# W_o of a hybrid retention block by seven products, its weight sums made in DRAM

## The chip, the cores and the metric

One core of one Trainium2 chip runs the whole layer in one launch. The metric is the device time of that launch in microseconds (us), the median of several runs. The engines are named as in the profile: PE is TensorE, DVE is VectorE, ACT is ScalarE, POOL is GpSimd, SP is SyncE, which here only issues DMAs.

## The reference

The layer takes x (512 tokens by 1024 features, float32). What matters for this change is the step that ends the token mixers:

```python
merged = jax.nn.sigmoid(gate_a) * y_a + jax.nn.sigmoid(gate_r) * y_r
x = x + merged @ w_o[l]                     # w_o: 1024 x 1024
h2 = rmsnorm(x, g_ffn[l])
x = x + (jax.nn.silu(h2 @ w_ff_gate[l]) * (h2 @ w_ff_up[l])) @ w_ff_down[l]
```

`y_a` is the output product of the short convolution (W_a_out, 1024 x 1024), `y_r` that of the retention (W_r_out, 2048 x 1024). In front of them stands one wide input projection; behind `x` comes the feed-forward part and a last RMSNorm.

## The kernel before, in words

**Precision.** All products are float32 by pairs: an operand t is held as hi (t rounded to the fast format) and lo = t - hi, and a product is the three matmuls hi·hi, hi·lo, lo·hi (`mm3`, L339 to L341; L380 and L424 in the other helpers). A weight piece of 128 x 1024 is loaded into a raw tile, ACT writes hi (L200), DVE writes lo (L201). There are ten raw tiles and five pairs of hi and lo; `take` keeps at least two pieces made ahead of the product that consumes them (AHEAD = 2), and their loads are issued four plan entries ahead (LEAD = 4).

**Seven products for eight.** Most of the projections are done by Winograd's form of Strassen's algorithm: both operands are cut into 2 x 2 quadrants, four sums of quadrants are formed on each side (s1 to s4 of the activations, t1 to t4 of the weights), and seven products of quadrants take the place of eight. `strassen` (L434 to L458) does it for token-major outputs: the products a11, s1, s2, a12, s3, a22, s4 in that order, each by `prod_tm` with 2 weight pieces and 24 matmuls of 512 columns, in three pairs of PSUM banks (a, d, b; there are eight banks). The weight sums t1 to t4 are made in SBUF by DVE adds (L298), except for the first two feed-forward quads (SUMMED), whose sums POOL's DMAs make in DRAM: a copy, then accumulating transfers (`sum_step`). There each of these is pinned behind a store of the same stage with `issue_after`.

**Order.** PLAN lists the weight pieces in order of consumption. The program is written in one order, and a list scheduler at build time may move an instruction ahead of others on its engine as soon as its inputs and its buffer are there; on the chip each engine runs its own list in order. Large activations live in fourteen `big` tiles.

**Around the change.** After the last product of W_r_out, `strassen(4, zf, ...)` computes y_a; its evictions `merge` (L967 to L971) multiply by the gate (L970) and add y_r (L971), behind the combining adds of `strassen` (L445, L450, L457). `turn(half)` (L974 to L984) transposes one half of the merged features, 16 transposes on PE, and splits them (L200, L201). W_o itself is not done by seven products: two halves of columns by two blocks of rows by four k by four token blocks, three matmuls each, all in eight banks; its last block is split into a `big` tile (`inbig`). The first two blocks run for all tokens, then each token block nb is finished in turn: `ev_o` (L999 to L1018) adds x (L1003), writes the row to DRAM, squares it on ACT (L1006) and scales it for the FFN (L1015); `tr_o` (L1020 to L1035) transposes it one block later (L1030) into the feed-forward operand. The feed-forward part starts with five products that need only the first 256 tokens (`first_tokens`); its own sums of activations come from `form` (L1162 to L1165: one DVE operation, one ACT cast, one DVE subtraction).

Of the kernel before, what the change touches and what calls it, by code (L numbers as in the profile page):

```python
# [53 lines left out]
WIDTH = {"w": 512, "x": 256, "a": 512, "f": 256, "d": 512}  # L54
# [96 lines left out]
SUMMED = (("f", 0), ("f", 1))  # L151


def loads():


    out = []
    for i, x in enumerate(PLAN):
        if x[0] == "q":
            _, quad, name, u, nk = x  # L160
            need = name if quad in SUMMED else NEEDS.get(name)
            if need:
                out.append((i, quad, need, u, nk * WIDTH[quad[0]]))
    return out + [(len(PLAN), quad, "b12", 0, 4 * WIDTH[quad[0]]) for quad in SUMMED]

# [6 lines left out]
def block_kernel(ctx: ExitStack, tc: tile.TileContext, xw0, xw, xT, xtok, wpack, wquad, cols, decs, rot, g_ffn, g_final, out):  # L172
# [51 lines left out]
    def unit(inbig=False):  # L224
        if inbig:
            t = bigtile(F32R)
            return t[:, 0:2, :].rearrange("p a b -> p (a b)"), t[:, 2:4, :].rearrange("p a b -> p (a b)")
# [4 lines left out]
    def prefetch_block(loads, splits, inbig):  # L232
# [8 lines left out]
        for c in range(2):  # L241
            hi, lo = unit(inbig)
# [8 lines left out]
    wsum = {(quad, f): dram.tile([P, QH], F32, name=f"{f}{quad[0]}{quad[1]}")  # L251
            for quad in SUMMED for f in ("t1", "t2", "t3", "t4")}

    def quarter(quad, name, u=0):
        return wquad[next(i for i, x in enumerate(QUARTERS) if x[1:4] == (quad, name, u))]

    steps = [(quad, f, g, add) for group in (
        (("t1", "b11", 0), ("t3", "b22", 0)), (("t1", "b12", 1), ("t3", "b12", 1)),
        (("t2", "t1", 0),), (("t2", "b22", 1),), (("t4", "t2", 0),), (("t4", "b21", 1),))
        for quad in SUMMED for f, g, add in group]  # L260

    def sum_step(behind=None):

        if steps:
            quad, f, g, add = steps.pop(0)
            src = wsum[quad, g] if g[0] == "t" else quarter(quad, g)
# [11 lines left out]
    def load_raws(upto):  # L278
        while loaded[0] < len(LOADS) and LOADS[loaded[0]][0] <= upto:
            _, quad, name, u, n = LOADS[loaded[0]]  # L280
            t = rawtile()
            src = wsum[quad, name] if name[0] == "t" else quarter(quad, name, u)
# [20 lines left out]
    def prefetch(first=False, loads=None, splits=None):  # L303
# [7 lines left out]
        if x[0] == "c":  # L311
            units = prefetch_block(loads, splits, x[1] == "w_o" and x[2] == 512 and x[4] == 512)
# [121 lines left out]
    def strassen(n, forms, ev11, ev21, ev22, ev12):  # L434
# [366 lines left out]
    def do_mix(s):  # L801
        us, c = [], bigtile()[:, 0:2, :]
        feature_major(xg, lambda m, ps: us.append(snap(ps)))
# [7 lines left out]
        def ev_b(m, ps):  # L811
            nc.vector.tensor_tensor(out=c[:, m], in0=ps, in1=c[:, m], op=ALU.mult)
        feature_major(xg, ev_b)
# [102 lines left out]
    def do_wr(h, yr):  # L916
# [3 lines left out]
        for half in range(2):  # L920
            def ev(nb, ps):
# [5 lines left out]
                if h == HEADS - 1:  # L927
                    nc.vector.tensor_tensor(out=t, in0=t, in1=sgr[half][:, nb, :], op=ALU.mult)
            token_major(yr, 0, 1, ev)
# [34 lines left out]
    mt = ([], [])  # L964

# [8 lines left out]
    def turn(half):  # L974
        hi, lo = bigtile(F32R), bigtile(F32R)
        mt[0].append(hi)
        mt[1].append(lo)
        for nb in range(NB):
# [6 lines left out]
    strassen(4, zf, merge(0, 0), merge(0, 2), merge(1, 2), merge(1, 0))  # L985
    turn(0)


# [8 lines left out]
    XF, xf32 = {}, {}  # L997

    def ev_o(nb, pss):  # L999
        ac = small.tile([P, 6], F32, tag="fin", name="ac")  # L1000
        for half in range(2):
            yt = y[half][:, nb, :]
            nc.vector.tensor_tensor(out=yt, in0=pss[half], in1=yt, op=ALU.add)  # L1003
            nc.sync.dma_start(ydr[nb * P:(nb + 1) * P, half * 512:(half + 1) * 512], yt)
            sq = t512()
            nc.scalar.activation(sq, yt, AF.Square, accum_out=ac[:, half:half + 1])  # L1006
        nc.vector.tensor_scalar(out=ac[:, 3:4], in0=ac[:, 0:1], scalar1=1.0 / D, scalar2=EPS,
                                op0=ALU.mult, op1=ALU.add)
# [3 lines left out]
        hs = []  # L1012
        for half in range(2):
            h = t512()
            nc.vector.scalar_tensor_tensor(out=h, in0=y[half][:, nb, :], scalar=ac[:, 5:6],  # L1015
                                           in1=gb[:, half * 512:(half + 1) * 512], op0=ALU.mult, op1=ALU.mult)
            hs.append(h)
        return hs  # L1018

    def tr_o(nb, hs):  # L1020
# [6 lines left out]
        for q in range(2):  # L1027
            ps = bank()
            for k in range(4):
                nc.tensor.transpose(ps[:, k * P:(k + 1) * P], hs[q][:, k * P:(k + 1) * P], ident)  # L1030
# [6 lines left out]
    po = [[bank() for _ in range(NB)]]  # L1037
    for half in range(2):
        c = Chunk()
        for k in range(4):  # L1040
            for nb in range(NB):
                mm3(po[half][nb], act_pair(mt, k, slice(nb * P, (nb + 1) * P)), c.w(k, 0, 512), k == 0, False)
        if half == 0:
            turn(1)
            po.append([bank() for _ in range(NB)])
    cs = [Chunk(), Chunk()]
    hs = [None] * NB
    for nb in range(NB):
        for half in range(2):
            for k in range(4):  # L1050
                mm3(po[half][nb], act_pair(mt, 4 + k, slice(nb * P, (nb + 1) * P)), cs[half].w(k, 0, 512),
                    False, k == 3)
        if nb:
            tr_o(nb - 1, hs[nb - 1])
        hs[nb] = ev_o(nb, [po[half][nb] for half in range(2)])
        if nb in (1, 3):

            prefetch()
# [103 lines left out]
    def form(name, o, in0, in1, op):  # L1162
        nc.vector.tensor_tensor(out=o, in0=in0, in1=in1, op=op)
        XF[name] = form_tile()
        split(o, *XF[name])  # L1165
# [5 lines left out]
    form("s1", a22, a21, a22, ALU.subtract)  # L1171
    first_tokens(*FIRST_PRODUCTS[2])
    form("s2", a22, a22, a11, ALU.subtract)
    first_tokens(*FIRST_PRODUCTS[3])
    form("s3", a21, a11, a21, ALU.subtract)
    first_tokens(*FIRST_PRODUCTS[4])
    form("s4", a12, a12, a22, ALU.add)
# [116 lines left out]
def pack_quads(w_in, w_a, gate, up, down):  # L1294

    out = np.zeros((len(QUARTERS), P, QH), np.float32)
    for i, (_, (kind, *q), name, u, n) in enumerate(QUARTERS):
# [3 lines left out]
        elif kind == "a":  # L1301

            w = w_a.reshape(4, 2, P, 2, 512)[u:u + n // 512, r, :, c]
        elif kind == "f":
# [50 lines left out]
```

## Time and profile before

| what | value |
|---|---|
| median of 3 runs | 1027.11 us (1026.5 to 1027.32) |
| the profiled execution, its own time | 1027.93 us |
| its span, first to last instruction | 1026.1 us |
| busy PE, DVE, ACT, POOL | 1018.1, 886.3, 535.5, 125.0 us |
| mean granted PE clock | 0.999 of 2.4 GHz |

Busy time of PE counts overlapping matmuls as one stretch, so a busy PE need not run at its peak. The chain of waits is followed back from the last instruction and says which engine set the end. A wait of an engine off that chain costs nothing by itself.

### The profile page before, as it was taken

To read this page: it belongs to the slowest core of one execution; us is meant where nothing else is said; L and a number is where in the kernel's file an instruction comes from. 1 tells how busy PE (TensorE), PEld (TensorE's weight loads), DVE (VectorE), ACT (ScalarE), POOL (GpSimd) and SP (SyncE) were. 2 spreads that over 40 slices of the span, in tenths; PEclk is the share of its full clock that TensorE was granted. 3 is DMA by queue.
4 is the path that set the end of the run, shared out by engine and by line. 5 is a ranking of instruction groups with operands and counts; after the bars stand their busy time and mean duration, and the time that the engine had idled before them with its cause. 6 is when DMAs were issued, how large, how long until landed. Compare 5 with 4: busy or idle time off the path is not lost.

```text
span 1026.1 us, 14780 instructions
## 1 busy us (share of the span) xinstructions
PE 1018.1 (99%) x5610; PEld 887.9 (87%) x5610; DVE 886.3 (86%) x1151; ACT 535.5 (52%) x728; POOL 125.0 (12%) x205
## 2 busy tenths in 40 slices
PE   9999999999999999999999999999999999999997
PEld 7888888888888998888888888889998999899986
DVE  7878998969798988797999998569998999889996
ACT  7547655553656455342542334356654565556554
POOL 0030231222212003202011000000002000110011
PEclk9999999999999999999999999999999999999999
DMA  9525597794767657828177525633318522663513
GB/s 346 195 83 183 172 299 211 213 312 153 255 203 238 254 200 256 323 81 314 52 277 285 208 94 176 236 102 121 122 44 220 177 87 83 193 156 103 164 29 96
DMA packets 51304, 187.66 MB, mean 183 GB/s; under 512 B 6880, under 2 KB 7008, under 8 KB 47264
## 3 DMA queue, kind: packets, MB, share of 16 engines
q1 hardware_dynamic: 36448, 133.19, 37.5%
q0 software_dynamic: 14496, 53.23, 17.5%
q8 instruction: 44, 0.72, 0.3%
q10 hardware_dynamic: 288, 0.29, 0.1%
q14 instruction: 28, 0.23, 0.1%
HBM read 148.14 MB, written 46.92 MB: 190 GB/s over the span
## 4 chain that ended last, share of the span: by engine, by line
PE 97%; DVE 1%; DMA 1%; issue 0%; POOL 0%; ACT 0%; POOLq 0%; DVEq 0%; ACTq 0%
PE bank L424 34%; PE bank L380 28%; PE bank L339 11%; PE bank L341 11%; PE bank L340 11%; DMA raw<-wquad 1%; PE bank L470 0%; PE bank L1030 0%; PE bank L981 0%; PE bank L655 0%; DVE wlo L201 0%; DVE raw L298 0%; DVE big L1229 0%; DVE t L445 0%; POOL fin L1219 0%
## 5 line engine op out<-in xcount | busy, mean ns | idle before, releaser
L200 ACT CAST whi<-raw 128x1024 fp32r<-128x1024 f32 (+2 forms) x291 | 294.5, 1028 | 278.7 <-PE bank L424 60.0
L201 DVE TENSOR_TENSOR wlo<-raw,whi 128x1024 fp32r<-128x1024 f32 (+2 forms) x292 | 343.9, 1193 | 81.6 <-ACT whi L200 81.1
L380 PE MATMUL bank<-xform,whi 128*128 128x256 f32 x1424 | 257.6, 284 | 0.2 <-ACT whi L200 0.2
L380 PEld LDWEIGHTS bank<-xform,whi 128*128 128x128 f32 x1424 | 222.4, 192 | 1.2 <-ACT t L431 0.5
L380 PE MATMUL bank<-xform,wlo 128*128 128x256 f32 x712 | 201.5, 283 | 0.0
L424 PE MATMUL bank<-whi,big 128*128 128x512 f32 x596 | 187.6, 390 | 0.0
L298 DVE TENSOR_TENSOR raw<-raw 128x1024 f32<-128x1024 f32 (+1 forms) x128 | 152.1, 1206 | 3.8 <-DMA raw<-wquad 2.8
L380 PEld LDWEIGHTS bank<-xform,wlo 128*128 128x128 f32 x712 | 136.8, 192 | 0.0
L424 PEld LDWEIGHTS bank<-whi,big 128*128 128x128 f32 x596 | 112.0, 188 | 23.8 <-ACT t L431 0.4
L424 PE MATMUL bank<-whi,xform 128*128 128x512 f32 x384 | 121.3, 390 | 0.0
L424 PE MATMUL bank<-wlo,big 128*128 128x512 f32 x298 | 116.2, 390 | 0.0
L431 ACT COPY t<-bank 128x512 f32<-128x512 f32 x105 | 61.0, 585 | 56.3 <-PE bank L380 29.7
L339 PE MATMUL bank<-big,whi 128*128 128x512 f32 x220 | 85.8, 390 | 0.0
L341 PE MATMUL bank<-big,wlo 128*128 128x512 f32 x220 | 85.7, 390 | 0.0
L340 PE MATMUL bank<-big,whi 128*128 128x512 f32 x220 | 85.7, 390 | 0.0
L424 PEld LDWEIGHTS bank<-whi,xform 128*128 128x128 f32 x384 | 72.1, 188 | 15.1 <-DVE xform L201 0.2
L424 PE MATMUL bank<-wlo,xform 128*128 128x512 f32 x192 | 74.8, 390 | 0.0
L339 PE MATMUL bank<-whi,big 128*128 128x512 f32 x176 | 69.0, 392 | 0.0
L340 PE MATMUL bank<-wlo,big 128*128 128x512 f32 x176 | 68.6, 390 | 0.0
L341 PE MATMUL bank<-whi,big 128*128 128x512 f32 x176 | 68.2, 390 | 0.0
L424 PEld LDWEIGHTS bank<-wlo,big 128*128 128x128 f32 x298 | 56.0, 188 | 11.4
L340 PEld LDWEIGHTS bank<-big,whi 128*128 128x128 f32 x220 | 41.3, 188 | 8.6
(205 smaller groups left out, 1394.8 us busy)
## 6 DMA issues: line engine op xcount, KB each, us to landing
raw<-wquad SPq DMA_DIRECT2D x132, 512.0 KB, 4.6
raw<-wpack SPq DMA_DIRECT2D x50, 512.0 KB, 5.3
z<-t POOLq DMA_DIRECT2D x24, 256.0 KB, 4.7
zform<-z POOLq DMA_DIRECT2D x6, 1024.0 KB, 6.0
v<-t POOLq DMA_DIRECT2D x16, 256.0 KB, 5.3
sg<-t POOLq DMA_DIRECT2D x16, 256.0 KB, 5.0
qh<-t POOLq DMA_DIRECT2D x16, 256.0 KB, 3.0
ql<-t POOLq DMA_DIRECT2D x16, 256.0 KB, 3.6
```

The source lines that it names most:

```text
L200: first = (round or nc.scalar.copy)(hi, src)
L201: nc.vector.tensor_tensor(out=lo, in0=src, in1=hi.bitcast(F32), op=ALU.subtract)
L298: nc.vector.tensor_tensor(out=t, in0=t, in1=raws[quad, more, u][:, 0:n], op=ALU.add)
L339: nc.tensor.matmul(ps, lh, rh, start=first, stop=False)
L340: nc.tensor.matmul(ps, lh, rl, start=False, stop=False)
L341: nc.tensor.matmul(ps, ll, rh, start=False, stop=last)
L380: nc.tensor.matmul(o, l[:, c], r[:, k], start=start and s == 0 and k == 0 and i == 0, stop=stop and k == 3 and i == 2, skip_group_check=True)
L424: nc.tensor.matmul(pss[tt], l, r[:, c], start=start and k == 0 and i == 0, stop=stop and k == n - 1 and i == 2, skip_group_check=True)
L431: nc.scalar.copy(t, ps)
```

## The change

W_o goes over to seven products of 24 matmuls, with its weight sums t1 to t4 made in DRAM by POOL's transfers as for the first two feed-forward quads: 16 more transfers, of which only the first two fall into calls of `sum_step` that pin them. `strassen` gets a hook `behind`, through which the convolution's output product now does three things between its own products: before a22 the quadrant a11 of the merged features is transposed; before s4 (its last) the quadrant a22 is transposed, W_o's first product a11 is run, quadrant a21 is transposed and s1 is formed. `strassen` of W_a_out moves behind the load of `y` (x token-major) in the program. The rest of W_o follows: s1, s2, a12, s4, s3, a22; each result is added to y by `join`, and `complete` does what `ev_o` did, token block by token block. Of the four `tr_o` two now stand before the first feed-forward product and two between the first three. `inbig` and the two explicit `prefetch` calls are dropped. `form` is the function of before with the dictionary as an argument.

```diff
-WIDTH = {"w": 512, "x": 256, "a": 512, "f": 256, "d": 512}
+WIDTH = {"w": 512, "x": 256, "a": 512, "o": 512, "f": 256, "d": 512}
...
-    for name in FORMS:
+    for kind, name in [("a", x) for x in FORMS[:6]] + [("o", "b11"), ("a", "b22")] + [
+            ("o", x) for x in ("t1", "t2", "b21", "b22", "t3", "t4")]:
         for u in (0, 2):
-            out.append(("q", ("a",), name, u, 2))
-    for r in (0, 512):
-        for c in (0, 512):
-            b("w_o", r, 4, c, 512)
+            out.append(("q", (kind,), name, u, 2))
...
-SUMMED = (("f", 0), ("f", 1))
+SUMMED = (("f", 0), ("f", 1), ("o",))
+
+
+def parts(quad):
+    return (0, 2) if quad == ("o",) else (0,)
...
-    steps = [(quad, f, g, add) for group in (
+    steps = [(quad, f, g, u, add) for quads in (SUMMED[:2], SUMMED[2:]) for group in (
         (("t1", "b11", 0), ("t3", "b22", 0)), (("t1", "b12", 1), ("t3", "b12", 1)),
         (("t2", "t1", 0),), (("t2", "b22", 1),), (("t4", "t2", 0),), (("t4", "b21", 1),))
-        for quad in SUMMED for f, g, add in group]
+        for quad in quads for f, g, add in group for u in parts(quad)]
...
-            with tc.issue_after(behind.ins):
+            with tc.issue_after(behind.ins) if behind else nullcontext():
                 if add:
-                    nc.gpsimd.dma_start(out=wsum[quad, f], in_=src, accum_op=ALU.add, max_dma_last_dim=4 * CH)
+                    nc.gpsimd.dma_start(out=wsum[quad, f, u], in_=src, accum_op=ALU.add, max_dma_last_dim=4 * CH)
                 else:
-                    nc.gpsimd.dma_start(wsum[quad, f], src)
+                    nc.gpsimd.dma_start(wsum[quad, f, u], src)
...
-    def strassen(n, forms, ev11, ev21, ev22, ev12):
+    def strassen(n, forms, ev11, ev21, ev22, ev12, behind=None):
...
+        if behind:
+            behind(5)
         prod_tm(n, forms["a22"], a, False, True)
         for tt in range(2):
             ev21(tt, a[tt])
+        if behind:
+            behind(6)
         prod_tm(n, forms["s4"], d, False, True)
...
     def do_mix(s):
         us, c = [], bigtile()[:, 0:2, :]
+        if s == 3:
+            sum_step()
+            sum_step()
...
+            sum_step()
+            sum_step()
             token_major(yr, 0, 1, ev)
...
+    def turn(half, th):
+        name = f"a{th + 1}{half + 1}"
...
+        if name != "a21":
+            M[name] = form_tile()
+        for tt in range(2):
             ps = bank()
             for k in range(4):
-                nc.tensor.transpose(ps[:, k * P:(k + 1) * P], sga[half][:, nb, k * P:(k + 1) * P], ident)
+                nc.tensor.transpose(ps[:, k * P:(k + 1) * P], sga[half][:, 2 * th + tt, k * P:(k + 1) * P], ident)
             ps = ps.rearrange("p (k t) -> p k t", k=4)
-            sl = slice(nb * P, (nb + 1) * P)
-            split(ps, hi[:, :, sl], lo[:, :, sl])
+            sl = slice(tt * P, (tt + 1) * P)
+            if name != "a21":
+                split(ps, *(t[:, :, sl] for t in M[name]))
+            nc.scalar.copy(m32[name][:, :, sl], ps)
+
+    def form(out, name, o, in0, in1, op):
+        nc.vector.tensor_tensor(out=o, in0=in0, in1=in1, op=op)
+        out[name] = form_tile()
+        split(o, *out[name])
...
+    def join(nb, half, ps, op=ALU.add):
+
+        yt = y[half][:, nb, :]
+        nc.vector.tensor_tensor(out=yt, in0=yt, in1=ps, op=op)
+
+    def complete(nb, half, last):
+        yt, ac = y[half][:, nb, :], acs[nb]
+        nc.sync.dma_start(ydr[nb * P:(nb + 1) * P, half * 512:(half + 1) * 512], yt)
+        nc.scalar.activation(t512(), yt, AF.Square, accum_out=ac[:, last:last + 1])
...
+    def behind(i):
+        if i == 5:
+            turn(0, 0)
+            return
+        turn(1, 1)
+        po["a"] = [bank(), bank()]
+        prod_tm(4, of(M["a11"]), po["a"], True, False, lambda tt: join(tt, 0, po["a"][tt]))
+        turn(0, 1)
+        form(M, "s1", m32["a22"], m32["a21"], m32["a22"], ALU.subtract)
+    strassen(4, zf, merge(0, 0), merge(0, 2), merge(1, 2), merge(1, 0), behind)
+    a, d, b = po["a"], [bank(), bank()], [bank(), bank()]
+    prod_tm(4, of(M["s1"]), d, True, False, lambda tt: join(2 + tt, 1, d[tt]))
+    form(M, "s2", m32["a22"], m32["a22"], m32["a11"], ALU.subtract)
+    turn(1, 0)
+    prod_tm(4, of(M["s2"]), a, False, False, lambda tt: join(tt, 1, a[tt], ALU.subtract))
+    form(M, "s4", m32["a12"], m32["a12"], m32["a22"], ALU.add)
...
+    prod_tm(4, of(M["a12"]), b, True, True, ev)
+    form(M, "s3", m32["a21"], m32["a11"], m32["a21"], ALU.subtract)
...
+    prod_tm(4, of(M["s4"]), d, False, True, ev)
...
+    prod_tm(4, of(M["s3"]), a, False, False, ev)
...
+    prod_tm(4, of(M["a22"]), a, False, True, ev)
...
     first_tokens(*FIRST_PRODUCTS[0])
+    tr_o(2)
     first_tokens(*FIRST_PRODUCTS[1])
-    tr_o(NB - 1, hs[NB - 1])
+    tr_o(3)
```

## Rows read from the trace of the kernel before

**Rows 1.** The page: span, and the busy time of each engine.

```profile
span 1026.1 us, 14780 instructions
PE 1018.1 (99%) x5610; PEld 887.9 (87%) x5610; DVE 886.3 (86%) x1151; ACT 535.5 (52%) x728; POOL 125.0 (12%) x205
```

**Rows 2.** The page's chain that ended last, by engine.

```profile
PE 97%; DVE 1%; DMA 1%; issue 0%; POOL 0%; ACT 0%; POOLq 0%; DVEq 0%; ACTq 0%
```

**Rows 3.** All waits of PE: who for whom, us in total, times, longest.

```profile
PE bank L470 <- DVE t L467: 1.4, 1, 1.4
PE bank L380 <- ACT whi L200: 0.2, 1, 0.2
```

**Rows 4.** The chain in order of time, longest pieces: start us, us, what.

```profile
1.45 4.45 PE bank L470 x10
...
602.38 38.08 PE bank L424 x168
640.46 1.75 PE bank L981 x16
...
677.61 0.87 PE bank L1030 x8
...
690.71 5.75 PE bank L380 x48
```

**Rows 5.** Groups of PE from 640.2 to 690.8, one of three lines.

```profile
L340 PE MATMUL bank<-wlo,big 128*128 128x512 f32 x48 | 18.8, 391 | 0.0
...
L340 PE MATMUL bank<-big 128*128 128x512 f32 x16 | 6.2, 390 | 0.0
```

**Rows 6.** Stretches: us, busy PE, PEld, DVE, ACT, POOL; PEclk, DMA share, GB/s.

```profile
602.20:640.30 38.10, 38.10 (x170) 31.51 (x169) 31.60 (x39) 17.93 (x20) 0.00 (x0) 1.00 0.41 134
640.30:690.70 50.40, 50.40 (x251) 41.72 (x250) 30.11 (x46) 22.25 (x40) 1.64 (x3) 1.00 0.50 173
```

**Rows 7.** Stretches of 5 us in the same columns.

```profile
632.00:637.00 5.00, 5.00 (x24) 4.14 (x23) 5.00 (x9) 2.11 (x2) 0.00 (x0) 1.00 0.50 183
...
662.00:667.00 5.00, 5.00 (x23) 4.13 (x22) 1.23 (x1) 1.05 (x1) 0.00 (x0) 1.00 0.55 190
```

**Rows 8.** Timeline of DVE, end of W_a_out: start us, us, what.

```profile
623.67 1.28 DVE L445 TENSOR_TENSOR t<-bank,t 128x512 f32<-128x512 f32 x2
624.87 1.28 DVE L970 TENSOR_TENSOR big<-t,big 128x512 f32<-128x512 f32 x2
...
627.28 2.36 DVE L201 TENSOR_TENSOR wlo<-raw,whi 128x1024 fp32r<-128x1024 f32 x2
629.55 1.37 DVE L450 TENSOR_TENSOR t<-bank,t 128x512 f32<-128x512 f32 x2
```

**Rows 9.** Groups from 596 to 700: the ACT cast of a weight piece.

```profile
L200 ACT CAST whi<-raw 128x1024 fp32r<-128x1024 f32 x24 | 25.1, 1052 | 44.8 <-PE bank L341 21.6 <-PE bank L424 15.7 <-DVE big L928 4.4
```

**Rows 10.** Timeline of DVE at the feed-forward part's forms.

```profile
700.02 2.47 DVE L1163 TENSOR_TENSOR big<-big 128x1024 f32<-128x1024 f32 x2
...
708.68 3.49 DVE L201 TENSOR_TENSOR xform<-big,xform 128x1024 fp32r<-128x1024 f32 x3
```

**Rows 11.** Timeline of SP and of POOL: an early load, a gap.

```profile
528.55 0.33 SPq L1193 DMA_DIRECT2D gf<-g_final  x1
...
381.08 0.72 POOL L626 DMA_DIRECT2D z<-t  x1 [52.08 <-ACT t L200]
```

**Rows 12.** DMA issues: count, KB each, median us to landing.

```profile
t1f<-wquad POOLq DMA_DIRECT2D x4, 512.0 KB, 7.7
...
t2f<-wquad POOLq DMA_DIRECT2D x2, 512.0 KB, 9.3
```

**Rows 13.** The first 20 us in stretches, columns as in rows 6.

```profile
0.00:10.00 10.00, 8.55 (x27) 5.21 (x28) 5.61 (x15) 5.82 (x11) 0.72 (x7) 1.00 0.82 281
10.00:20.00 10.00, 10.00 (x46) 8.29 (x45) 9.90 (x16) 9.46 (x17) 0.00 (x0) 1.00 1.02 405
```

**Rows 14.** Timeline of ACT, the first weight casts that wait for a load.

```profile
19.48 1.05 ACT L200 CAST whi<-raw 128x1024 fp32r<-128x1024 f32 x1 [0.54 <-DMA raw<-wpack]
```

More of the change, by code (lines that the diff above doesn't have):

```diff
@@ L1 @@
-from contextlib import ExitStack
+from contextlib import ExitStack, nullcontext
 import numpy as np
@@ L163, in loads @@
                 out.append((i, quad, need, u, nk * WIDTH[quad[0]]))
-    return out + [(len(PLAN), quad, "b12", 0, 4 * WIDTH[quad[0]]) for quad in SUMMED]
+    return out + [(len(PLAN), quad, "b12", u, QH) for quad in SUMMED for u in parts(quad)]
 LOADS = loads()
@@ L222, in block_kernel, with unit @@
     ready = []
[L224 to L227, printed above, removed]
+    def unit():
         hi = wpool.tile([P, QH], F32R, tag="whi", name="whi")
@@ L230, in unit, with prefetch_block @@
         return hi, lo
-    def prefetch_block(loads, splits, inbig):
+    def prefetch_block(loads, splits):
         i = block[0]
@@ L241, in prefetch_block @@
         for c in range(2):
-            hi, lo = unit(inbig)
+            hi, lo = unit()
             units.append((hi, lo))
@@ L249, in block_kernel, with quarter @@
     raws = {}
-    wsum = {(quad, f): dram.tile([P, QH], F32, name=f"{f}{quad[0]}{quad[1]}")
-            for quad in SUMMED for f in ("t1", "t2", "t3", "t4")}
-    def quarter(quad, name, u=0):
+    wsum = {(quad, f, u): dram.tile([P, QH], F32, name="_".join(map(str, (f, u, *quad))))
+            for quad in SUMMED for u in parts(quad) for f in ("t1", "t2", "t3", "t4")}
+    def quarter(quad, name, u):
         return wquad[next(i for i, x in enumerate(QUARTERS) if x[1:4] == (quad, name, u))]
-    steps = [(quad, f, g, add) for group in (
+    steps = [(quad, f, g, u, add) for quads in (SUMMED[:2], SUMMED[2:]) for group in (
         (("t1", "b11", 0), ("t3", "b22", 0)), (("t1", "b12", 1), ("t3", "b12", 1)),
         (("t2", "t1", 0),), (("t2", "b22", 1),), (("t4", "t2", 0),), (("t4", "b21", 1),))
-        for quad in SUMMED for f, g, add in group]
+        for quad in quads for f, g, add in group for u in parts(quad)]
     def sum_step(behind=None):
         if steps:
-            quad, f, g, add = steps.pop(0)
-            src = wsum[quad, g] if g[0] == "t" else quarter(quad, g)
-            with tc.issue_after(behind.ins):
+            quad, f, g, u, add = steps.pop(0)
+            src = wsum[quad, g, u] if g[0] == "t" else quarter(quad, g, u)
+            with tc.issue_after(behind.ins) if behind else nullcontext():
                 if add:
-                    nc.gpsimd.dma_start(out=wsum[quad, f], in_=src, accum_op=ALU.add, max_dma_last_dim=4 * CH)
+                    nc.gpsimd.dma_start(out=wsum[quad, f, u], in_=src, accum_op=ALU.add, max_dma_last_dim=4 * CH)
                 else:
-                    nc.gpsimd.dma_start(wsum[quad, f], src)
+                    nc.gpsimd.dma_start(wsum[quad, f, u], src)
     def rawtile():
@@ L281, in load_raws @@
             t = rawtile()
-            src = wsum[quad, name] if name[0] == "t" else quarter(quad, name, u)
+            src = wsum[quad, name, u] if name[0] == "t" else quarter(quad, name, u)
             nc.sync.dma_start(t[:, 0:n], src[:, 0:n])
@@ L311, in prefetch @@
         if x[0] == "c":
-            units = prefetch_block(loads, splits, x[1] == "w_o" and x[2] == 512 and x[4] == 512)
+            units = prefetch_block(loads, splits)
         else:
@@ L972, in merge @@
         return ev
[L974 to L978, printed above, removed]
+    M, m32 = {}, {}
+    def turn(half, th):
+        name = f"a{th + 1}{half + 1}"
+        if not m32:
+            t = [bigtile(), bigtile()]
+            for j in range(4):
+                m32[f"a{j // 2 + 1}{j % 2 + 1}"] = t[j // 2][:, j % 2 * 2:j % 2 * 2 + 2, :].rearrange(
+                    "p a (b c) -> p (a b) c", c=256)
+        if name != "a21":
+            M[name] = form_tile()
+        for tt in range(2):
             ps = bank()
             for k in range(4):
-                nc.tensor.transpose(ps[:, k * P:(k + 1) * P], sga[half][:, nb, k * P:(k + 1) * P], ident)
+                nc.tensor.transpose(ps[:, k * P:(k + 1) * P], sga[half][:, 2 * th + tt, k * P:(k + 1) * P], ident)
             ps = ps.rearrange("p (k t) -> p k t", k=4)
-            sl = slice(nb * P, (nb + 1) * P)
-            split(ps, hi[:, :, sl], lo[:, :, sl])
-    strassen(4, zf, merge(0, 0), merge(0, 2), merge(1, 2), merge(1, 0))
-    turn(0)
+            sl = slice(tt * P, (tt + 1) * P)
[6 more added lines that the diff above has]
+        split(o, *out[name])
     y = [bigtile(), bigtile()]
@@ L997, in block_kernel @@
     XF, xf32 = {}, {}
[L999 to L1008, printed above, removed]
+    acs = [small.tile([P, 6], F32, tag="fin", name="ac") for _ in range(NB)]
+    hs = [None] * NB
+    def join(nb, half, ps, op=ALU.add):
[5 more added lines that the diff above has]
+        nc.scalar.activation(t512(), yt, AF.Square, accum_out=ac[:, last:last + 1])
+        if not last:
+            nc.vector.tensor_scalar(out=ac[:, 3:4], in0=ac[:, 0:1], scalar1=1.0 / D, scalar2=EPS,
+                                    op0=ALU.mult, op1=ALU.add)
+            return
         nc.vector.scalar_tensor_tensor(out=ac[:, 4:5], in0=ac[:, 1:2], scalar=1.0 / D,
@@ L1011, in ev_o, with tr_o @@
         nc.gpsimd.tensor_tensor(out=ac[:, 5:6], in0=ac[:, 4:5], in1=mhalf[:, 0:1], op=ALU.pow)
[L1012 to L1020, printed above, removed]
+        hs[nb] = [t512(), t512()]
+        for j, h in enumerate(hs[nb]):
+            nc.vector.scalar_tensor_tensor(out=h, in0=y[j][:, nb, :], scalar=ac[:, 5:6],
+                                           in1=gb[:, j * 512:(j + 1) * 512], op0=ALU.mult, op1=ALU.mult)
+    def tr_o(nb):
         th, o = nb // 2, (nb % 2) * P
@@ L1035, in tr_o @@
             nc.vector.tensor_tensor(out=lo, in0=ps, in1=hi.bitcast(F32), op=ALU.subtract)
[L1037 to L1058, printed above, removed]
+    po = {}
+    def behind(i):
+        if i == 5:
+            turn(0, 0)
+            return
+        turn(1, 1)
[3 more added lines that the diff above has]
+        form(M, "s1", m32["a22"], m32["a21"], m32["a22"], ALU.subtract)
@@ new lines, in block_kernel, with ev @@
+    strassen(4, zf, merge(0, 0), merge(0, 2), merge(1, 2), merge(1, 0), behind)
[5 more added lines that the diff above has]
+    form(M, "s4", m32["a12"], m32["a12"], m32["a22"], ALU.add)
+    def ev(tt):
+        join(tt, 0, b[tt])
+        complete(tt, 0, 0)
@@ new lines, in block_kernel, with ev @@
+    prod_tm(4, of(M["a12"]), b, True, True, ev)
+    form(M, "s3", m32["a21"], m32["a11"], m32["a21"], ALU.subtract)
+    def ev(tt):
+        join(tt, 1, d[tt])
+        complete(tt, 1, 1)
+    prod_tm(4, of(M["s4"]), d, False, True, ev)
+    def ev(tt):
+        join(2 + tt, 1, a[tt], ALU.subtract)
+        complete(2 + tt, 1, 0)
+        if tt == 0:
+            tr_o(0)
+    prod_tm(4, of(M["s3"]), a, False, False, ev)
+    def ev(tt):
+        join(2 + tt, 0, a[tt])
+        complete(2 + tt, 0, 1)
+        if tt == 0:
+            tr_o(1)
@@ L1160, in down @@
                  lambda tt, t: add_y(t, 2 + tt, 1), lambda tt, t: add_y(t, tt, 1))
[L1162 to L1165, printed above, removed]
     first_tokens(*FIRST_PRODUCTS[0])
+    tr_o(2)
     first_tokens(*FIRST_PRODUCTS[1])
-    tr_o(NB - 1, hs[NB - 1])
+    tr_o(3)
     a11, a12, a21, a22 = xf32[0, 0], xf32[1, 0], xf32[0, 1], xf32[1, 1]
-    form("s1", a22, a21, a22, ALU.subtract)
+    form(XF, "s1", a22, a21, a22, ALU.subtract)
     first_tokens(*FIRST_PRODUCTS[2])
-    form("s2", a22, a22, a11, ALU.subtract)
+    form(XF, "s2", a22, a22, a11, ALU.subtract)
     first_tokens(*FIRST_PRODUCTS[3])
-    form("s3", a21, a11, a21, ALU.subtract)
+    form(XF, "s3", a21, a11, a21, ALU.subtract)
     first_tokens(*FIRST_PRODUCTS[4])
-    form("s4", a12, a12, a22, ALU.add)
+    form(XF, "s4", a12, a12, a22, ALU.add)
     for q0, n in FF_PARTS:
@@ L1291, in pack_weights, with pack_quads @@
     return out
-def pack_quads(w_in, w_a, gate, up, down):
+def pack_quads(w_in, w_a, w_o, gate, up, down):
     out = np.zeros((len(QUARTERS), P, QH), np.float32)
```

10 lines of the change are left out of this document (7 added, 3 removed).

## The prediction

> **What bounds the kernel now.** I read the page first: PE is busy for 1018.1 of 1026.1 us, DVE for 886.3 [rows 1]. Busy PE can hide idle gaps, so the chain comes second: 97% of it is PE [rows 2], and the table of waits has only two waits of PE for another engine, 1.4 us at the start and 0.2 us later [rows 3]. The reader should see that nothing else ends late: the time is the number of matmuls times their pace, and it falls only when PE gets less work and still waits for nobody. The pace is in the chain in order of time: the seven products of W_a_out, 168 matmuls of 512 columns, take 38.08 us, 0.2267 us each, 5.44 us for a product of 24 [rows 4]. W_o then lasts from 640.46 to the first feed-forward product at 690.71, 50.25 us [rows 4].
>
> **What is removed.** W_o has 192 matmuls of 512 columns: 48 and 16 on each of three lines [rows 5]. At 0.2267 that is 43.52 us; seven products of 24 are 168, or 38.08 us. Saved on PE: 24 × 0.2267 = 5.44 us. The transposes stay: 32 of the merged features (two groups of 16 at 1.75 us) and 32 of `tr_o` (four groups of 8 at 0.87 us) [rows 4], now in smaller groups. Check: 43.52 + 2 × 1.75 + 3 × 0.87 = 49.63, so 0.62 us of the 50.25 is the slow start behind five groups. The new order has six groups in the stage and one more behind the first feed-forward product; at 0.12 us a group I add 0.2 us, between a gain of 0.6 (no slow start) and a loss of 0.6.
>
> **What is added on DVE.** The pace there is the distance of starts: 0.60 us for an operation of 512 columns, 1.135 us for one of 1024 [rows 8]. W_o's weights become 14 pieces instead of 8, six more lo: 6.8 us. Results joined to y: 14 instead of 8, 3.6 us. Four forms s1 to s4 of two DVE operations of 1024 columns: 9.1 us. The lo of quadrant a21 goes: −1.2 us. Together 18.3 us. ACT gets six casts at 1.05 us [rows 9], four for the forms and eight copies of the merged features, less two casts; it is busy 22.25 of 50.40 us there [rows 6], so I charge nothing; without that cover it is part of the chain priced below.
> DVE is busy 30.11 of the stage's 50.40 us [rows 6]: 20.3 are free, 14.9 once PE is 5.44 shorter. So 18.3 us don't fit by 3.4 us, and the rest must find room behind 690 or in the earlier gaps, where five weight buffers limit how far ahead it can be done. Nor are the free spots where the new work first falls due: DVE is full from 632 to 637 and nearly idle from 662 to 667 [rows 7].
>
> **The tightest place** is the product s2. In PE's new order it comes, after W_a_out's a12 ends at 602.38 + 4 × 5.44 = 624.1, behind five products and four turned quadrants (8 transposes, 0.87 us each): 5 × 5.44 + 4 × 0.87 = 30.7 us later. Due on DVE by then: the gate, sum and combining operations of W_a_out, 22 × 0.60 = 13.2; eight weight pieces, 9.1; the lo of two quadrants, 2.4; four joins, 2.4; forms s1 and s2, 4.5. Sum 31.6 us against 30.7: 0.9 us late even if DVE never pauses. s2's own chain is s1's end, join 0.60, form 1.135, cast 1.05, lo 1.135 = 3.9 us if the scheduler leaves it where the program has it; less the transposes beside it (0.87) PE would wait 3.05 us. I don't expect that order, because the four forms of the feed-forward part, written between products 6 us apart, already start together from 700.02 on [rows 10], as soon as their inputs are there. So I take 1.0 us, near the budget's excess, with 0 and 3.05 as ends. The other forms have a whole product between their writing and their use (s1: 5.44 us for about 4.5), so I charge nothing there; if DVE's backlog lasts, up to 1.5 us.
>
> **What moves.** y's load (two of 1 MB on SP) goes ahead of W_a_out; it needs two `big` tiles, which the last W_r_out evictions leave about when W_a_out starts; loads on SP behind it are four plan entries early, so nothing. Dropping `inbig` and the two `prefetch` calls: at 690 each piece has a product of 6 us to be made in, so nothing, at worst one cast and lo, 2.2 us, inside the range. `complete` issues the same eight stores of y on SP, and only loads with that lead queue behind them. The later `tr_o` keep their PE time.
>
> **The sums in DRAM.** Sixteen transfers of 512 KB; such a one lands after 7.7 us, an accumulating one after up to 9.3 [rows 12], and nothing of W_o is due before 620. On POOL's queue a transfer that adds waits until the copy before it has landed, and the stores behind it wait too; but that chain starts only behind the last pinned step near 328, and POOL then does nothing until 381.08, 52 us [rows 11], so six links of 9 us fit. Nothing; without the gap, late stores of z, a few us. Fourteen loads for eight in W_o at a DMA share of 0.50 [rows 6]: nothing.
> The two copies that begin t3 and the two additions behind them wait for nothing at all, and nothing pins them. Loads without inputs are issued early here: that of g_final went out at 528.55 [rows 11], although the program has it at its end. I expect these four near the start, where the DMA share is 0.82 and then 1.02 at 405 GB/s [rows 13]. They move 2.1 MB, 5.2 us at that rate; that is the upper end, 0 the lower. I take 0: the first cast held up by a weight load, by 0.54 us at 19.48 [rows 14], is of the second head's weights, which PE needs some 6 us later.
> The Trainium skill (DMA: Bandwidth & Descriptors, Issuing engines are not separate DMA queues) says that transfers issued from SP, ACT and POOL run on the same 16 engines and interleave. The share of 1.02 agrees that there is no room left at 10 to 20 us; by that rule alone the four would cost up to their 5.2 us.
>
> **Sum**, against the profiled execution of 1027.93 us (span 1026.1 and 1.83 around it): −5.44 + 0.2 + 1.0 = −4.2, so 1023.7. The median shown is 0.8 below that execution: 1022.9 us. A measurement of this kernel tells about 0.2% (2.05 us) from no change.
>
> **Rivals.**
> *A, the forecast*, 0.70: PE's work counts, a short wait at s2. With its ends 1021.2 to 1024.9.
> *B, DVE becomes the bound of the stage*, 0.14. For it: the 3.4 us that don't fit and 5 us stretches already full [rows 7]. Against it: the same table's idle ones behind 660. Waits of 3.05 at s2 and 1.5 at the later forms take most of the 5.44: 1027.1 − 5.44 + 0.2 + 4.55 = 1026.4, within 0.2%; with half of the second, faster by a little more than the bound.
> *C, the early sums hold up the start*, 0.07: up to 5.2 us more, 1023 to 1028. It decides if weights of the first head, not the second, come late. For it the full DMA engines [rows 13], against it the casts' slack [rows 14].
> *D, slower*, 0.07: PE waits the full 3.05 us for s2, its clock falls, and the next product runs at half pace. The granted clock is 1.00 in every stretch of these rows [rows 6, 7, 13], so no row has the fall itself; but the ten first matmuls, of 512 columns after an idle PE, took 4.45 us, 0.445 each, about twice 0.2267 [rows 4]. One product at that pace costs 5.44 us more: 1022.9 − 1.0 + 3.05 + 5.44 = 1030.4. It decides only if the form of s2 is issued behind the last join of s1 and PE has nothing else to run. Against it: PE's list can be filled with the next product, and the waits of before are short [rows 3].
> The Trainium skill (TensorE: Matmul & The Clock Gate, Part 1) states the rule behind D: an idle TensorE is throttled to half its clock, and activity releases it.
> That the change doesn't do what it says (no fewer matmuls) is left with 0.02, about 1027.
>
> **How the numbers follow.** Faster by over 0.2% (below 1025.06): A and 0.06 of B and C, 0.76. Slower (above 1029.16): D and a worse B, 0.08. Same: 0.16. The predicted time is A's. The range goes from A's lower end up over B's price, 1021.2 to 1026.5, and leaves out D and the worst of C.
>
> **What would show it.** Right: the distance from W_a_out's first matmul to the first feed-forward product is 88.3 us before [rows 4] and 84.2 or less after, with one `tr_o` fewer in it (0.87 of that moves, so 83.3); 168 matmuls of 512 columns in W_o; granted clock 1.00; DVE above 90% from 625 to 685; the wait that is late next is PE's for the lo of s2 (DVE) or for its hi (ACT). B would show PE waits at s2 and at s4 or s3 of together over 3 us; C a wait of PE before 30 us and POOL's copies issued before 10 us; D a granted clock below 1 near 655. Wrong altogether: a W_o stage shorter by 4 us or more with the same end time, which would put the loss in the stretch from 330 to 600.

## The result, and the profile after

The changed kernel takes 1032.32 us (median of 5 runs, 1031.04 to 1033.17) against 1027.11 us: a ratio of 1.005, interval 1.0039 to 1.0061. It is slower by 5.2 us, where the forecast was 4.2 us faster. The profiled execution has a span of 1030.4 us and a mean granted clock of 0.995.

The page of the changed kernel, busy times and the chain by engine, to be read beside [rows 1, 2]:

```profile
span 1030.4 us, 14816 instructions
PE 1017.2 (99%) x5586; PEld 885.4 (86%) x5586; DVE 903.7 (88%) x1169; ACT 548.9 (53%) x744; POOL 137.3 (13%) x221
...
PE 95%; DVE 2%; DMA 1%; issue 0%; SPq 0%; ACT 0%; POOL 0%; POOLq 0%; DVEq 0%
```

The 24 matmuls are gone (5586 for 5610), and DVE has 17.4 us more. But PE is 95% of the chain now instead of 97%, and DVE 2% instead of 1%. The longest waits of PE in the changed kernel, beside [rows 3]:

```profile
PE bank L338 <- ACT whi L202: 2.5, 1, 2.5
PE bank L423 <- ACT xform L202: 2.1, 1, 2.1
PE bank L473 <- DVE t L470: 1.4, 1, 1.4
...
```

Two waits of over 2 us are new, one for a weight's hi, one for the hi of an activation form. The chain of the changed kernel in order of time says where they lie (start us, us, what):

```profile
3.79 14.97 DMA raw<-wpack
...
78.23 152.57 PE bank L423 x672
...
607.50 27.20 PE bank L423 x120
...
659.71 0.33 issue
660.04 1.23 DVE big L1006
661.29 1.05 ACT xform L202
662.39 20.92 PE bank L423 x84
...
765.88 29.17 PE bank L423 x126
```

Two more pieces of the same view of the kernel before give the marks to measure from:

```profile
73.20 152.47 PE bank L424 x672
...
760.85 14.18 PE bank L424 x62
```

Between these marks, W_a_out's first matmul (602.38 before [rows 4], 607.50 after) and the spans, the budget is (the last column is the run e6_spread_s2 below):

| stretch | before | after | e6 |
|---|---|---|---|
| start to the piece of 672 matmuls | 73.20 | 78.23 | 72.52 |
| from there to W_a_out | 529.18 | 529.27 | 529.05 |
| W_a_out, W_o, first feed-forward part | 158.47 | 158.38 | 155.15 |
| from the first down product to the end | 265.25 | 264.52 | 264.58 |

So 5.0 us are lost in the first 78 us, and the stretch of the change itself, 24 matmuls shorter, gains 0.1 us. The 0.7 us of the last row contain the 0.2 us wait of before [rows 3], which is not there after. As for single executions: the runs below without early transfers reach the piece of 672 at 72.5 (e5, e6, e8) or at 73.3 (e1, e3), so 0.7 us between two of them means nothing.

**The start.** The timeline of POOL in the changed kernel shows the four sums that nothing pins:

```profile
1.31 0.72 POOL L270 DMA_DIRECT2D t_o<-wquad  x1 [0.33 <-issue]
2.38 0.55 POOL L270 DMA_DIRECT2D t_o<-wquad  x1
7.35 0.86 POOL L268 DMA_DIRECT2D t_o<-wquad  x1 [4.42 <-DMA t_o<-wquad]
8.86 0.81 POOL L268 DMA_DIRECT2D t_o<-wquad  x1 [0.65 <-DMA t_o<-wquad]
```

Stretches of the changed kernel in the columns of [rows 6]: two of the start, one of W_o.

```profile
15.00:20.00 5.00, 2.51 (x12) 1.77 (x11) 2.16 (x4) 3.08 (x5) 0.00 (x0) 1.00 0.99 301
20.00:25.00 5.00, 4.47 (x13) 3.27 (x14) 5.00 (x7) 4.65 (x8) 0.00 (x0) 0.66 1.02 419
...
660.00:670.00 10.00, 7.88 (x30) 6.22 (x28) 8.82 (x10) 4.38 (x7) 0.00 (x0) 0.83 0.56 189
```

PE runs out of work after 17 us, because a weight load issued at 3.79 lands 14.97 us later. Right behind the wait the granted clock falls from 2.4 to 1.2 GHz for part of 20 to 25 us (a share of 0.66 on average there), with matmuls 0.43 us apart.

**The product s2.** The timeline of DVE in the changed kernel:

```profile
658.57 0.68 DVE L1025 TENSOR_TENSOR big<-big,bank 128x512 f32<-128x512 f32 x1
659.44 0.69 DVE L1025 TENSOR_TENSOR big<-big,bank 128x512 f32<-128x512 f32 x1 [0.19 <-PE bank L423]
660.04 1.22 DVE L1006 TENSOR_TENSOR big<-big 128x1024 f32<-128x1024 f32 x1
```

The form s2 (L1006) is issued right behind the last join of s1 (L1025), in the order of the program. PE is idle for the last 2.12 us before 662.39 and then goes on at half its clock for a while, as the 0.83 of 660 to 670 shows.

### The profile page after: what moved, and what is told of

Its sections match the earlier page's. It is cut to its first block, busy times and chain, and to the rows that moved or that the text cites. A ratio compares the mean times of both kernels' runs of the same rounds, so it can differ in the third digit from the quotient of the medians.

```text
span 1030.4 us, 14816 instructions
## 1 busy us (share of the span) xinstructions
PE 1017.2 (99%) x5586; PEld 885.4 (86%) x5586; DVE 903.7 (88%) x1169; ACT 548.9 (53%) x744; POOL 137.3 (13%) x221
## 4 chain that ended last, share of the span: by engine, by line
PE 95%; DVE 2%; DMA 1%; issue 0%; SPq 0%; ACT 0%; POOL 0%; POOLq 0%; DVEq 0%
PE bank L423 40%; PE bank L379 27%; PE bank L340 10%; PE bank L339 10%; PE bank L338 10%; DMA raw<-wpack 1%; DVE big L1006 1%; DVE wlo L203 0%; PE bank L1053 0%; PE bank L998 0%; DVE xform L203 0%; DVE big L1270 0%; SPq L503 0%; POOL fin L1260 0%; ACT xform L202 0%
## 5 line engine op out<-in xcount | busy, mean ns | idle before, releaser
L202 ACT CAST whi<-raw 128x1024 fp32r<-128x1024 f32 (+2 forms) x299 | 302.8, 1028 | 274.8 <-PE bank L423 68.8
L203 DVE TENSOR_TENSOR wlo<-raw,whi 128x1024 fp32r<-128x1024 f32 (+2 forms) x300 | 352.9, 1191 | 75.1 <-ACT whi L202 74.5
L423 PE MATMUL bank<-whi,big 128*128 128x512 f32 x596 | 187.5, 390 | 0.0
L423 PE MATMUL bank<-whi,xform 128*128 128x512 f32 x496 | 158.1, 393 | 2.1 <-ACT xform L202 2.1
L423 PE MATMUL bank<-wlo,big 128*128 128x512 f32 x298 | 116.0, 389 | 0.0
L423 PEld LDWEIGHTS bank<-whi,xform 128*128 128x128 f32 x496 | 93.6, 189 | 22.4 <-ACT xform L202 2.4
L423 PE MATMUL bank<-wlo,xform 128*128 128x512 f32 x248 | 97.3, 393 | 0.0
L423 PEld LDWEIGHTS bank<-wlo,xform 128*128 128x128 f32 x248 | 47.1, 190 | 9.8
L338 PEld LDWEIGHTS bank<-big,whi 128*128 128x128 f32 x220 | 41.7, 190 | 11.6 <-ACT whi L202 2.9
L340 PEld LDWEIGHTS bank<-big,wlo 128*128 128x128 f32 x220 | 41.7, 189 | 9.5 <-DVE wlo L203 1.0
L338 PE MATMUL bank<-whi,big 128*128 128x512 f32 x128 | 49.8, 389 | 0.0
```

What stands on the lines that cost most here:

```text
L202: first = (round or nc.scalar.copy)(hi, src)
L203: nc.vector.tensor_tensor(out=lo, in0=src, in1=hi.bitcast(F32), op=ALU.subtract)
L338: nc.tensor.matmul(ps, lh, rh, start=first, stop=False)
L340: nc.tensor.matmul(ps, ll, rh, start=False, stop=last)
L423: nc.tensor.matmul(pss[tt], l, r[:, c], start=start and k == 0 and i == 0, stop=stop and k == n - 1 and i == 2, skip_group_check=True)
```

## The experiments

Each is timed against the kernel before. Medians in us and ratios with their 95% intervals:

| run | this | before | ratio |
|---|---|---|---|
| e1_pin | 1031.95 | 1027.4 | 1.0043 (1.0031 to 1.0056) |
| e2_s2 | 1029.84 | 1027.4 | 1.0025 (1.0015 to 1.0036) |
| e3_both | 1029.36 | 1027.4 | 1.0021 (1.0012 to 1.003) |
| e4_early | 1033.14 | 1027.4 | 1.0055 (1.0043 to 1.0068) |
| e5_spread | 1026.27 | 1026.75 | 0.9995 (0.9987 to 1.0004) |
| e6_spread_s2 | 1023.29 | 1026.75 | 0.9967 (0.9954 to 0.9979) |
| e7_later | 1023.5 | 1026.75 | 0.9968 (0.9956 to 0.998) |
| e8_dve | 1034.85 | 1026.75 | 1.0078 (1.0065 to 1.0091) |
| e9_two | 1027.72 | 1027.17 | 1.0005 (0.9996 to 1.0014) |
| e10_four | 1032.8 | 1027.17 | 1.0051 (1.0037 to 1.0065) |

My theory after the result was that two separate losses hide the gain: the four early sums take DMA time from the first weights, and s2's form comes too late on DVE. The rival was that the stage is bound by DVE (rival B), so that moving either would give nothing.

**e1_pin: the unpinned sums behind the last pinned step, near 325 us.**

```diff
+    pin = [None]
...
-            with tc.issue_after(behind.ins) if behind else nullcontext():
+            pin[0] = behind or pin[0]
+            with tc.issue_after(pin[0].ins):
```

> Changed kernel, but every sum step without a pin of its own is issued after the last pinned store of the gate quads (about 325 us). Theory (four of the DRAM sums, issued from 1.3 us on, hold up the first weights and with them the whole kernel by 5.1 us): W_a_out's first matmul comes back from 607.5 to about 602.4 us and the time from 1032.3 to about 1027.2. Rival (the loss is VectorE's alone, in the W_o stage): the time stays within 0.5 us of 1032.3. Either way the wait at W_o's product s2 (2.1 us) and the clock of 0.5 behind it stay.

The start is as before (the piece of 672 begins at 73.34), but the time hardly falls, and W_a_out begins no earlier. The chain and PE's waits of this kernel, and three of its stretches (columns of [rows 6]):

```profile
73.34 152.55 PE bank L426 x672
...
354.42 28.48 DMA raw<-wpack
...
608.78 27.20 PE bank L426 x120
```

```profile
PE bank L382 <- ACT t L433: 4.0, 1, 4.0
```

```profile
360.00:380.00 20.00, 20.00 (x165) 19.78 (x164) 17.45 (x23) 9.50 (x12) 2.63 (x4) 1.00 1.02 336
380.00:384.00 4.00, 0.59 (x3) 0.17 (x1) 0.82 (x1) 1.00 (x2) 0.00 (x0) 0.83 1.01 349
384.00:388.00 4.00, 3.42 (x16) 3.42 (x17) 3.03 (x4) 1.05 (x3) 1.47 (x2) 0.50 1.01 415
```

All sixteen transfers are now issued between 320 and 375 us. POOL has the time for them, the sixteen DMA engines have not: their share is 1.02, a weight load takes 28.48 us, and PE waits 4.0 us, with the granted clock at 0.50 behind it. From the piece of 672 to W_a_out it takes 535.44 us, 6.2 more than the changed kernel. The loss has moved, not gone. A full share by itself is no loss: the changed kernel, with twelve of the transfers here, has 1.04 over 340 to 360 us without a wait of PE; the four more are too many.

**e2_s2: the form s2 ahead of the product s1.**

```diff
+    form(M, "s2", m32["a22"], m32["a22"], m32["a11"], ALU.subtract)
     prod_tm(4, of(M["s1"]), d, True, False, lambda tt: join(2 + tt, 1, d[tt]))
-    form(M, "s2", m32["a22"], m32["a22"], m32["a11"], ALU.subtract)
```

> Changed kernel, but form s2 of W_o is written ahead of product s1 instead of behind it; nothing else. Theory (s2 waits because its form is queued behind the last join of s1, and the clock falls behind that wait): 2.7 us of gap and about 1.1 us of half clock go, time about 1028.6, granted clock 1.00 from 600 to 700. Rival (VectorE is over-full, whichever order): the wait comes back at a later product and the time stays at 1031 to 1032.

It takes 2.5 us off the changed kernel, where I expected 3.7. The wait for the hi of s2 is gone, and the stretch from W_a_out to the first down product is 155.21 us (158.38 after). The waits of the start stay.

**e3_both: e1 and e2 together.**

> Changed kernel with both: sums pinned and form s2 ahead of product s1. Theory: the two losses add, 1032.3 - 5.1 - 3.8 = 1023.4, about 0.36% faster than the kernel before. Rival (VectorE over-full): 1026 to 1027.

The stretch of W_o is right again (155.19 us), and the wait near 380 stays:

```profile
PE bank L382 <- ACT t L433: 4.0, 2, 3.7
```

1029.36 us, 6 more than I expected. So pinning alone does not rescue the sums; the place must have free DMA engines.

**e4_early: the kernel before with four transfers near the start and nothing else.** Two copies of 512 KB between places in DRAM and an accumulating transfer behind each; nothing reads them, and the rest of the computation is that of the kernel before.

```diff
+        if s == 3:
+            for i in (0, 1):
+                t = dram.tile([P, QH], F32, name=f"x{i}")
+                nc.gpsimd.dma_start(t, wquad[40 + i])
+                nc.gpsimd.dma_start(out=t, in_=wquad[42 + i], accum_op=ALU.add, max_dma_last_dim=4 * CH)
```

> Kernel before, with nothing of the change but four unused transfers of 512 KB in DRAM (two copies, two accumulating), unpinned, as the changed kernel issues them. Theory: they alone cost the start, 1027.1 + 5.1 = about 1032.2, and the first weights wait as in the changed kernel. Rival (the start is late for another reason): within 1 us of 1027.1.

It loses 5.7 us without any part of W_o's change; its piece of 672 begins at 79.00. PE's waits in this kernel, two of them new:

```profile
PE bank L559 <- ACT t L200: 2.0, 1, 2.0
...
PE bank L560 <- DVE t L201: 1.1, 1, 1.1
```

The loss is put at other instructions than in the changed kernel, yet is as large: unused transfers alone cost it, by making loads late, and whichever load comes late stops PE. The DMA share is 1.00 over 5 to 30 us; whether the engines or the memory behind them are short of time is not separated here, and the share alone does not tell, as it is 1.02 in the kernel before too [rows 13].

**e5_spread: the unpinned sums behind POOL's last step of heads 0 and 1, near 435 and 487 us.** There the DMA share before was 0.43 (430 to 510 us).

```diff
+    pin = [None]
...
+            with tc.issue_after((behind or pin[0]).ins):
...
+            pin[0] = nc.gpsimd.tensor_tensor(out=mv[:, 3:4], in0=mv[:, 2:3], in1=mhalf[:, 0:1], op=ALU.pow)
...
-            sum_step()
-            sum_step()
+            for _ in range(4):
+                sum_step()
```

> Changed kernel, but the 14 unpinned DRAM sums are issued after the last POOL operation of the first two retention heads (about 435 and 487 us), where the DMA engines of the kernel before are busy for 0.16 to 0.31 (430 to 460) and 0.15 to 0.18 (490 to 510) of the time. Theory (a sum costs only what it takes from loads that are about to be late): no wait of TensorE at the start nor near 380, W_a_out begins at 602.4 to 603, time about 1027.2; the wait at s2 and its slow clock stay. Rival (the sums cost some 4 to 5 us wherever they stand, by their mere volume): 1031 to 1032.

One stretch of this kernel, then the longest wait of PE that is left:

```profile
430.00:510.00 80.00, 80.00 (x355) 66.24 (x354) 71.72 (x113) 34.03 (x49) 20.51 (x33) 1.00 0.81 244
```

```profile
PE bank L425 <- ACT xform L202: 2.1, 1, 2.1
...
```

The share rises to 0.81, PE is busy for all 80 us, and 6.05 us of the changed kernel's time are gone. What remains is s2: from W_a_out at 601.72 to the first down product at 759.96, 158.24 us.

**e6_spread_s2: e5 and e2 together.**

> The same with form s2 ahead of product s1. Theory: the stage from W_a_out's start to the first down product is 155.2 us, as in the runs with form s2 moved, against 158.5 in the kernel before: 3.3 us faster than before, about 1024.0. Rival (VectorE is over-full and gives back what one wait loses): 1026 to 1027.

1023.29 us, faster than both kernels: 3.5 us under the kernel before, 9.0 under the changed one. Its chain at the marks of the budget, and its waits of PE:

```profile
72.52 152.35 PE bank L425 x672
...
601.57 27.21 PE bank L425 x120
...
756.72 29.16 PE bank L425 x126
```

```profile
PE bank L475 <- DVE t L472: 1.4, 1, 1.4
PE bank L1055 <- DVE t L1042: 0.3, 1, 0.3
PE bank L381 <- ACT t L432: 0.3, 1, 0.3
```

The timelines of DVE show the form of s2, in e5 first and then in e6 (W_a_out starts within 0.15 us in both):

```profile
653.70 0.69 DVE L1027 TENSOR_TENSOR big<-big,bank 128x512 f32<-128x512 f32 x1 [0.23 <-PE bank L425]
654.30 1.22 DVE L1008 TENSOR_TENSOR big<-big 128x1024 f32<-128x1024 f32 x1
```

```profile
644.36 2.48 DVE L1008 TENSOR_TENSOR big<-big 128x1024 f32<-128x1024 f32 x2
...
647.36 1.21 DVE L203 TENSOR_TENSOR xform<-big,xform 128x1024 fp32r<-128x1024 f32 x1
...
650.89 1.22 DVE L1008 TENSOR_TENSOR big<-big 128x1024 f32<-128x1024 f32 x1
```

The pair at 644.36 can only be s1 and s3: s2 is written over s1's tile and must let s1's lo (647.36) read it first, and s4 needs s2 and a quadrant that is turned only from 653.32 on. So the form at 650.89 is that of s2, 3.4 us earlier than in e5 and no longer behind the last join (653.70 there).

The two losses add up: e5 takes 6.05 us off, the move of s2 another 2.98 (medians; that of the kernel before differs by 0.4 between the two sets of runs). That excludes B as the main cause: with the same DVE work (903.6 us of busy time, 903.7 after) the time falls by 9 us.

**e7_later: e6 with the third `tr_o` behind the second feed-forward product.** It tries whether the small waits near 700 come from the transposes' place.

```diff
 first_tokens(*FIRST_PRODUCTS[0])
-    tr_o(2)
 first_tokens(*FIRST_PRODUCTS[1])
+    tr_o(2)
```

> The same, and the third transposed token block of y moves behind the second feed-forward product, beside the fourth. Theory (its transposes wait for VectorE's scaled rows and share out badly between the first two products): about 1 us less than the kernel without this move. Rival (the first feed-forward products are limited by weight casts, not by these transposes): no difference within 0.5 us.

1023.5 us, no difference that can be measured from e6. The place of that transpose is not the limit.

**e8_dve: e2's order, W_o's weight sums by DVE adds in SBUF, no transfers in DRAM.**

```diff
-SUMMED = (("f", 0), ("f", 1), ("o",))
+SUMMED = (("f", 0), ("f", 1))
```

> Changed kernel with form s2 ahead of product s1, but W_o's weight sums made by VectorE as for the other quads (eight more additions of 128x1024, 1.14 us each) and none of the 16 DRAM transfers. Theory (VectorE has no room in this stage): the start is as in the kernel before, W_a_out begins at 602.4, but 9 us of VectorE work more in a full stage cost TensorE 3 to 8 us there: 1027 to 1031. Rival (VectorE's load is no limit, only its order was): 1023.5 to 1024.5, as good as sums in DRAM at the best place.

8.1 us slower than the kernel before, 11.6 slower than e6, for 8.4 us more DVE work (912.0 us), and well above the 1031 that I had as the upper end. The two longest new waits of PE in this kernel, and two of its stretches:

```profile
PE bank L423 <- DVE wlo L203: 2.0, 2, 1.1
PE bank L379 <- ACT xform L1056: 1.8, 1, 1.8
...
```

```profile
650.00:660.00 10.00, 7.75 (x32) 5.90 (x32) 10.00 (x12) 6.97 (x8) 0.00 (x0) 0.88 0.00 1
...
680.00:690.00 10.00, 6.97 (x33) 5.05 (x32) 9.56 (x14) 9.32 (x16) 1.46 (x1) 0.91 0.88 296
```

DVE is full, while the DMA share is 0.00 in the first of these stretches, so there it is not the DMA engines that hold up PE: the further DVE work comes out of PE's time, with a fallen clock on top (0.88, 0.91). So rival B names a real limit, one that the changed kernel is near; in this order, without the sums in DRAM, seven products do not pay here.

**e9_two and e10_four: what sets the price of early transfers.** The kernel before with two, and with four, unused plain copies of 512 KB; the rest of the computation is that of the kernel before.

```diff
+        if s == 3:
+            for i in (0, 1):
+                t = dram.tile([P, QH], F32, name=f"x{i}")
+                nc.gpsimd.dma_start(t, wquad[40 + i])
```

(e10 has `range(4)`.)

> The kernel before with only two unused copies of 512 KB from DRAM to DRAM, issued near the start, no accumulating transfers (the output does not use them). The run with two copies and two accumulating transfers lost 5.7 us. If the price goes by the bytes moved on full DMA engines, two copies cost half of it, 2.5 to 2.9 us, 1029.3 to 1030.3. If it is the accumulating transfers that hold up the loads, two copies cost under 1 us, below 1028. If one copy at the very start is enough to make the first weights late, nearly the whole 5 us, near 1032.

> The kernel before with four unused copies of 512 KB from DRAM to DRAM, none accumulating (the output does not use them). The copies wait for nothing, so all four go out within 5 us of the start, where the accumulating ones waited for the copies and went out up to 19 us. By bytes it costs the same as two copies and two accumulating transfers, 5.2 to 5.8 us, 1032 to 1033.3. If accumulating transfers are dearer, it stays below 1031. If being issued earlier, ahead of more of the first loads, is dearer, above 1034.

Two copies cost 0.55 us (the interval includes nothing at all), four cost 5.6. So the price is not proportional to the bytes. By e9 alone the accumulating transfers could be the dear ones; e10 shows that none is needed, since four plain copies cost what two copies and two accumulating transfers cost in e4. (Its four are all issued in the first 4 us, those of e4 up to 19 us; that the two differences cancel is not excluded.) The wait in each kernel, on PE's timeline, e9 first:

```profile
10.73 0.50 PE L339 MATMUL bank<-big,whi 128*128 128x512 f32 x1 [1.15 <-ACT whi L200]
```

```profile
13.58 0.50 PE L339 MATMUL bank<-big,whi 128*128 128x512 f32 x1 [2.85 <-ACT whi L200]
```

The stretches 10 to 15 us of e9 and 15 to 20 us of e10 hold what follows that wait:

```profile
10.00:15.00 5.00, 4.27 (x19) 3.42 (x20) 4.09 (x9) 4.73 (x11) 0.00 (x0) 1.00 1.02 365
```

```profile
15.00:20.00 5.00, 5.00 (x18) 4.01 (x17) 5.00 (x11) 5.00 (x10) 0.00 (x0) 0.74 1.02 399
```

With two copies PE waits 1.15 us and goes on at the full clock; with four it waits 2.85 us and the clock is at 0.74 behind it. So there is some slack in the first loads, and beyond it a wait costs itself and then the slower matmuls behind it.

## Why the prediction was wrong

**The work on PE: right.** 24 matmuls fewer, at the same pace. With both losses taken away (e6), the stretch from W_a_out to the first down product is 3.32 us shorter; the forecast's −5.44 + 0.2 + 1.0 was −4.24. Its 1.0 was for a wait at s2 that e6 does not have, so against −5.44 + 0.2 = −5.24 there are 1.9 us missing. In e6 PE's busy time falls short by 0.84 us between 670 and 720 us, where DVE is busy for 9.45 of every 10 us, and counted from start to start five gaps between 675 and 711 us hold 1.7 us more than PE's pace. That this is the 3.4 us of DVE work that "don't fit" is likely, but was not tested: of the two waits that the table still has there, one is for DVE and one for ACT, 0.3 us each.

**The work on DVE: right.** 18.3 us forecast, 17.4 measured.

**The early sums: the step that failed most.** "I take 0", with 5.2 as the upper end. The place was right (POOL issues all four before 10 us), and the price was the upper end: 5.0 us in the budget, 5.7 by e4. I argued from one row, a cast held up by 0.54 us whose weights PE needs 6 us later [rows 14], that there was slack. But the loads behind the four all come late: the first cast of a 128 x 1024 piece starts at 18.78 us instead of 13.10, the third at 25.40 instead of 19.48. Slack is spent once: e9 shows it covering most of two transfers, e10 that it does not cover four. And I priced only the transfers' time, not the clock. That the sum comes out near 5.2 all the same is luck, as e9 shows: half the bytes cost a tenth. In the changed kernel nine matmuls from 19.88 to 24.22 us, less the 0.53 us of a second wait, take 3.81 us where 2.04 would do, so 1.8 of the 5 us are the clock's.
The Trainium skill (DMA: Bandwidth & Descriptors, Issuing engines are not separate DMA queues) has all issuers share the same 16 engines. The runs agree where the share is at 1.0: at the start in e4 and e10, near 360 us in e1.

**The product s2: the second step that failed.** "I don't expect that order" was wrong. I took 1.0 us for the wait. The full 3.05 us chain was there; PE's idle time was 2.12 us by the table of waits and 2.7 by the chain. I had inferred from four forms that start together [rows 10] that the scheduler would bring s2's form forward too. It brought that of s3 forward, written last of the four (the pair in e6's DVE rows is in e5 too, at 644.52), but left s2's behind the join, although e6 shows that it can run 3.4 us earlier. That s2 is written over s1's tile, and so becomes ready only behind s1's lo, may be why; that was not tried. Rival D, at 0.07, named the mechanism with its place, and only its second part was too large: not a whole product at half pace (5.44 us) but eight matmuls from 662.39 to 665.91, 3.52 us for 1.81, 1.7 us more. Wait and slow matmuls are 3.8 us; moving the form gives back 2.98 (e5 to e6), so some 0.8 of it is lost again later in the stretch.
The Trainium skill (TensorE: Matmul & The Clock Gate, Part 1) has the clock fall to half when PE is idle; the granted 0.50 behind both waits agrees.

**What moves, and POOL's queue: right, with a flaw.** From the piece of 672 matmuls to W_a_out nothing changed (529.18, 529.27), so y's early load and the sums behind the last pinned step cost nothing in the changed kernel. But the reason given, that six links fit POOL's gap [rows 11], looked at the wrong resource. In e1 four transfers more at that place cost 6.2 us, 4.0 of it a wait, with POOL's time to spare and the DMA engines full.

**The chances.** C and D were weighed as alternatives at 0.07 each. They are independent, in different stages, and both came: e6's −3.32 with both losses put back, 5.0 at the start and 3.0 at s2, is +4.7. The spans show +4.3 (the last row of the budget gives 0.7 back) and the medians +5.2; the difference between these two is mostly that the profiled execution of before lay 0.8 above its median.

## What to carry to other kernels

A transfer that depends on nothing was issued here as soon as the program started, where the first loads had room for little more: pin such transfers to a stretch whose DMA share has room for all of them (0.43 before, in e5), and read that share, not the issuing queue's idle time. Write an operation on the critical product as early as its inputs allow, and do not count on a scheduler to move it. Price an idle PE as the wait plus the slower matmuls behind it, and add rivals that sit in different stages instead of choosing between them.

## What the runs showed of the hardware

- After idle times of PE of 2.12 and 2.49 us (the changed kernel) and 2.85 us (e10) the granted clock was 0.50 for a while; after one of 1.15 us (e9) it stayed at 1.00. In e8 two idle times of 1.18 and 1.06 us, with 0.7 us of work between them, brought it to 0.50 too. The slow matmuls behind the waits of 2.12 and 2.49 us cost 1.7 and 1.8 us more than at full pace, about three quarters of the waits themselves.
- Two plain 512 KB copies within DRAM at the start cost 0.55 us, four cost 5.6, two copies with two accumulating transfers 5.7.
- With the DMA share at 1.02, a 512 KB weight load took 28.48 us (e1); the median of such loads (`raw<-wpack`) in the kernel before is 5.3 us.
